# Two of the five taps of a depthwise convolution as matmuls with diagonal weights

## The chip, the cores and the metric

The kernel runs on one core of one Trainium2 chip. Its time is the device time of one execution in microseconds (us). PE is TensorE, DVE is VectorE, ACT is ScalarE, POOL is GpSimd, SP issues the DMAs. PSUM is the memory that matmuls write; the kernel divides it into banks of 128 partitions by 512 float32 values.

## The reference

One layer of a hybrid encoder for 2048 tokens of width 1024: a modulated RMSNorm, one input projection, then two branches side by side (a state-space branch "S5" and a gated DeltaNet branch), an output projection, the residual and a final RMSNorm. The change lies in the DeltaNet branch, where queries, keys and values pass a centred convolution of five taps along the tokens, each channel by itself, and a SiLU:

```python
def centred_depthwise_conv(t, w):            # w: (5, 1536), one weight per tap and channel
    ch = t.shape[-1]
    return lax.conv_general_dilated(
        t, w[:, None, :].astype(t.dtype), window_strides=(1,),
        padding=[(CONV_K // 2, CONV_K // 2)],
        dimension_numbers=("NWC", "WIO", "NWC"), feature_group_count=ch)

proj = h @ w_in
u_a, z_a, qkv, z_b, beta_fb, alpha_fb = jnp.split(proj, [o1, o2, o3, o4, o5], axis=-1)
qkv = jax.nn.silu(centred_depthwise_conv(qkv, conv_w))
q, k, v = jnp.split(qkv, 3, axis=-1)
```

Keys and queries are then normalised per head of 128 channels; the rest of the branch runs later in the kernel.

## The kernel before, in words

The program has three parts in time: a start (norm, modulation, the first columns of the projection), the projection stage, which is the one that the change touches (about 250 to 745 us of the trace), and the DeltaNet chunks with the output projection after it.

In the projection stage the columns of `w_in` are done as jobs of 128 columns: three gate jobs, one job of 16 columns, four key jobs (K1 to K4, `kind` 1), four query jobs (Q1 to Q4, `kind` 0), and then value jobs (V1 to V4, `kind` 2) that alternate with gate jobs (Z). A job has four rounds, one for each block of 512 tokens. A round is one product of 24 float16 matmuls of 128x512 into a bank `gm` (three for each of eight slices of the 1024 inputs: high parts, and the two cross terms with the low parts), the eviction by ACT, and one `tick`.

The order of everything else is written out by hand: each engine works through its instructions in the order in which the Python code emits them. `later(n, f, rank)` puts `f` into the n-th tick from now; a tick runs what is due, sorted by rank, and then one step of `side`, a generator that carries the S5 branch along: first its parameters (long chains of small DVE operations), then eight tables (`s5_tables`: transposes `sq<-ident,bpw` and small products `sq<-cpw,bbr` and `sq<-cpw,bbi`), then sixteen batches (`s5_in`: `sq<-uT,bpt` and four DVE products; in the next tick `s5_out` of the batch before: `sq<-uT,tt` and `sq<-w,cpt`, and `s5_scan`: four DVE scans into `xs` and three DVE operations, the first of which writes a bank).

For each block a key, query or value job runs: `evac` (ACT copies the product, scaled, into `raw`, which holds 2048 tokens with two zeros at either end), two ticks later `tap` (ACT writes `raw` times the first tap's weight into `cv`), one tick later `conv` (DVE adds four taps by `scalar_tensor_tensor`, the first three results in a PSUM bank, the last in `cv`), one tick later `gated` (SiLU). Keys go on through `total` (sum of squares by matmuls), `taken`, a `rsqrt` chain on DVE once per job, and `turn` (transposes), values through `turn`.

Banks come from one pool: two with the tag `gm`, three `pt`, three `sq`. The convolution shares the three `sq` banks with the S5 tables and batches; a matmul into a bank whose last reader has not finished waits, and so does all of PE behind it. The weights of the next job are split into `wh` (ACT) and `wl` (DVE, line 223) while the present one runs.

Of the kernel before, what the change touches and what calls it, by code (L numbers as in the profile page):

```python
# [9 lines left out]
F32 = mybir.dt.float32  # L10
# [5 lines left out]
AF = mybir.ActivationFunctionType  # L16
# [15 lines left out]
def mm(nc, out, lhsT, rhs, start=True, stop=True):  # L32
    nc.tensor.matmul(out, lhsT, rhs, start=start, stop=stop)  # L33


def bc(ap, n):
    return ap.unsqueeze(2).to_broadcast([ap.shape[0], ap.shape[1], n])
# [3 lines left out]
def block(ctx, tc, x, c, ada_w, ada_b, norm_w, w_in, conv_w,  # L41
# [4 lines left out]
    nc = tc.nc  # L46
    V, A, P = nc.vector, nc.scalar, nc.gpsimd
# [28 lines left out]
    def select(name, src, pattern, base, cm, op=ALU.is_ge):  # L76
        t = const.tile([128, 128], F32, name=name)
        P.affine_select(out=t, in_=src, pattern=pattern, compare_op=op, fill=0.0, base=base, channel_multiplier=cm)
        return t

    def pool(name, bufs=1, side="left", **kw):
        return tc.tile_pool(name=name, bufs=bufs, side=side, reuse_waits="tile", **kw)
# [4 lines left out]
    def bank(tag, shape=(128, 512)):  # L87
        return psum.tile(list(shape), F32, tag=tag, name=tag, bufs=PS_BUFS[tag])

    ident = select("ident", ones, [[-1, 128]], 0, 1, op=ALU.is_equal)  # L90
# [17 lines left out]
    def rsqrt(pool, dst, src, tag):  # L108

        shp = list(src.shape)  # L110
        y = pool.tile(shp, F32, tag=tag + "y", name=tag + "y")
        t = pool.tile(shp, F32, tag=tag + "t", name=tag + "t")
        V.tensor_scalar(out=t.bitcast(I32), in0=src.bitcast(I32), scalar1=1, scalar2=None,
                        op0=ALU.arith_shift_right)
        V.tensor_scalar(out=y.bitcast(I32), in0=t.bitcast(I32), scalar1=-1.0,
                        scalar2=float(0x5F3759DF), op0=ALU.mult, op1=ALU.add)
        for it in range(3):
            V.tensor_tensor(out=t, in0=y, in1=y, op=ALU.mult)
            V.scalar_tensor_tensor(out=t, in0=t, scalar=-0.5, in1=src, op0=ALU.mult, op1=ALU.mult)
            V.scalar_tensor_tensor(out=(dst if it == 2 else y), in0=t, scalar=1.5, in1=y,  # L120
                                   op0=ALU.add, op1=ALU.mult)
# [52 lines left out]
    cw = s5t.tile([128, 12, 5], F32, name="cw")  # L174
# [794 lines left out]
    tp = p1.enter_context(pool("tp", 2))  # L969
# [5 lines left out]
    def later(n, fn, rank=0):  # L975
        late.append((clock[0] + n, fn, rank))
# [9 lines left out]
    def job(i, evac):  # L986
        w = w_done(i)
        for tb in range(NB):
            ps = gemm(w, tb)
            evac(tb, ps, w[2])  # L990
            if tb == 0:
                w_dma(i + 2)
                mx, cut = w_max(i + 1), w_cut(i + 1)
                next(mx, None)
            elif tb == 1:
                whole(mx)
            else:
                next(cut, None)
                next(cut, None)
            tick()  # L1000
# [8 lines left out]
    def conv_job(i, kind, h):  # L1009
        i12 = kind * 4 + h  # L1010
        raw = rp.tile([128, L + 4], F32, tag="big", name="raw")
        V.memset(raw[:, 0:2], 0.0)
        V.memset(raw[:, L + 2:L + 4], 0.0)
        cvs = {}
        if kind == 1:
            ss, rk = [sp.tile([128, NCH], F32, tag=t, name=t, bufs=2) for t in ("kss", "rk")]

        def evac(tb, ps, iv):
            A.activation(out=raw[:, 2 + tb * 512:2 + (tb + 1) * 512], in_=ps, func=AF.Copy, scale=iv)  # L1019
            if tb:  # L1020
                later(1, lambda: tap(tb - 1))
            if tb == NB - 1:
                later(2, lambda: tap(tb))

        def tap(tb):
            cv = cvs[tb] = tp.tile([128, 512], F32, tag="cv", name="cv", bufs=9)
            A.activation(out=cv, in_=raw[:, tb * 512:tb * 512 + 512], func=AF.Copy, scale=cw[:, i12, 0:1])  # L1027
            later(1, lambda: conv(tb))

        def conv(tb):  # L1030

            cv, ps = cvs[tb], bank("sq")
            o = tb * 512
            for j in range(1, 5):
                V.scalar_tensor_tensor(out=cv if j == 4 else ps, in0=raw[:, o + j:o + j + 512],  # L1035
                                       scalar=cw[:, i12, j:j + 1], in1=cv if j == 1 else ps,
                                       op0=ALU.mult, op1=ALU.add)
            later(1, lambda: gated(tb))

        def gated(tb):  # L1040
            cv = cvs[tb]
            A.activation(out=cv, in_=cv, func=AF.Silu)
            if kind == 0:
                nc.sync.dma_start(out=qT_d[:, tb * 4:tb * 4 + 4, h, :], in_=cv.rearrange("p (c t) -> p c t", t=128))
            if kind == 2:
                later(1, lambda: turn(tb))
                return
            sq = tp.tile([128, 512], F32, tag="sq", name="sq")
            A.activation(out=sq, in_=cv, func=AF.Square)
            later(1, lambda: total(tb, sq), 2)  # L1050

        def total(tb, sq):

            ps = bank("pt")
            for j in range(4):
                mm(nc, ps[:, j:j + 1], sq[:, j * 128:(j + 1) * 128], ones[:, 0:1])
            later(1, lambda: taken(tb, ps), 1)

        def taken(tb, ps):
            c4 = slice(tb * 4, tb * 4 + 4)  # L1060
            if kind == 0:

                V.tensor_scalar(out=iq2[:, c4, h], in0=ps[:, 0:4], scalar1=EPS, scalar2=128.0 * EPS,
                                op0=ALU.add, op1=ALU.mult)
                cvs.pop(tb)
                return
            V.tensor_scalar(out=ss[:, c4], in0=ps[:, 0:4], scalar1=EPS, scalar2=None, op0=ALU.add)
            if tb == NB - 1:

                rsqrt(sp, rk, ss, "rk")  # L1070
                for n in range(NB):
                    later(1 + n, lambda n=n: turn(n), 2)

        def turn(tb):
            c4 = slice(tb * 4, tb * 4 + 4)
            cv = cvs.pop(tb)
            ps = bank("pt")
            for j in range(4):
                nc.tensor.transpose(ps[:, j * 128:(j + 1) * 128], cv[:, j * 128:(j + 1) * 128], ident)  # L1079
            if kind == 2:  # L1080
                vt = tp.tile([128, 4, 128], F32, tag="z", name="vt", bufs=3)
                A.activation(out=vt, in_=ps, func=AF.Copy)
                nc.sync.dma_start(out=vt_d[:, c4, h, :], in_=vt)
                return
            later(1, lambda: norm(ps, c4), 1)

        def norm(ps, c4):
            kt = tp.tile([128, 4, 128], F32, tag="kt", name="kt", bufs=3)
            V.tensor_tensor(out=kt, in0=ps.rearrange("p (c d) -> p c d", d=128), in1=bc(rk[:, c4], 128), op=ALU.mult)
            nc.sync.dma_start(out=kt_d[:, c4, h, :], in_=kt)  # L1090
            later(2, lambda: back(kt, c4), 1.5)

        def back(kt, c4):
            ps = bank("pt")
            for j in range(4):
                nc.tensor.transpose(ps[:, j * 128:(j + 1) * 128], kt[:, j, :], ident)
            kk = tp.tile([128, 4, 128], F32, tag="z", name="kk", bufs=3)
            A.activation(out=kk, in_=ps, func=AF.Copy)
            nc.sync.dma_start(out=kT_d[:, c4, h, :], in_=kk)

        job(i, evac)

    def ab_job(i):
# [162 lines left out]
    for c0, n in order[NU:]:  # L1266
        if (c0, n) in ZA:
            z_job(i, za_d[:, ZA.index((c0, n)), :])
        elif (c0, n) in ZB:
            z_job(i, zb_d[:, ZB.index((c0, n)), :])  # L1270
        elif n == 16:
            ab_job(i)
        else:
            kind, h = divmod((c0 - 1024) // 128, 4)
            conv_job(i, kind, h)
        i += 1
# [588 lines left out]
```

## Time and profile before

| | |
|---|---|
| median of 3 runs | 1396.05 us (1393.25 to 1398.34) |
| the profiled execution | 1399.54 us, span of its trace 1397.8 us |
| mean granted TensorE clock | 0.959 |
| PE busy | 1283.2 us, 92% of the span |
| DVE busy | 1000.4 us, 72% |
| ACT busy | 672.1 us, 48% |
| POOL busy | 703.7 us, 50% |

A busy time is the sum over one engine's instructions, overlaps counted once. Matmuls are pipelined: each is shown longer than the distance to the next one, so the pace of PE is read from the distance between starts. PEld is the loading of the stationary operand, which runs beside the matmuls. PEclk is the clock that TensorE was granted as a share of its full speed. In a timeline each row has its start, its length, engine, line, operation, output and inputs, shape and count, and in brackets the idle time before it with what ended it.

### The profile page before, as it was taken

To read this page: it belongs to the slowest core of one execution; us is meant where nothing else is said; L and a number is where in the kernel's file an instruction comes from. 1 tells how busy PE (TensorE), PEld (TensorE's weight loads), DVE (VectorE), ACT (ScalarE), POOL (GpSimd) and SP (SyncE) were. 2 spreads that over 40 slices of the span, in tenths; PEclk is the share of its full clock that TensorE was granted. 3 is DMA by queue.
4 is the path that set the end of the run, shared out by engine and by line. 5 is a ranking of instruction groups with operands and counts; after the bars stand their busy time and mean duration, and the time that the engine had idled before them with its cause. 6 is when DMAs were issued, how large, how long until landed. Compare 5 with 4: busy or idle time off the path is not lost.

```text
span 1397.8 us, 26533 instructions
## 1 busy us (share of the span) xinstructions
PE 1283.2 (92%) x9936; PEld 902.9 (65%) x9936; DVE 1000.4 (72%) x2095; ACT 672.1 (48%) x1348; POOL 703.7 (50%) x680
## 2 busy tenths in 40 slices
PE   2879897898999999999998789999999988998997
PEld 2445343354665555555554679999998877887885
DVE  4636479877765899889865677888888555865664
ACT  4445321444654555344446566777666423432332
POOL 3214223655541478878731765656653235654443
PEclk9789998999999999999999899999999999999998
DMA  9445342222457434353525423444435487686533
GB/s 313 169 93 180 96 83 84 66 80 83 117 170 186 134 113 144 91 163 100 150 74 150 147 77 116 152 145 138 132 111 197 144 289 276 226 309 211 181 111 108
DMA packets 255280, 206.43 MB, mean 148 GB/s; under 512 B 88496, under 2 KB 206256, under 8 KB 255152
## 3 DMA queue, kind: packets, MB, share of 16 engines
q1 hardware_dynamic: 255152, 204.75, 47.5%
q8 instruction: 78, 1.28, 0.4%
q14 instruction: 50, 0.41, 0.1%
HBM read 133.38 MB, written 73.33 MB: 148 GB/s over the span
## 4 chain that ended last, share of the span: by engine, by line
PE 70%; DVE 16%; DMA 4%; issue 3%; ACT 2%; POOL 2%; SPq 1%; DVEq 0%; POOLq 0%; ACTq 0%
PE gm L33 38%; PE sq L33 16%; PE pt L33 12%; DVE sq L1035 3%; DVE w L510 1%; DVE tm L510 1%; DVE xs L939 1%; PE pt L1079 1%; DMA of<-o_d 1%; DVE t L510 1%; DVE wl L223 1%; PE sq L1752 1%; DMA xt<-in_x_dram 1%; DMA ay_d<-ytx 1%; DVE pb L1423 0%
## 5 line engine op out<-in xcount | busy, mean ns | idle before, releaser
L33 PE MATMUL gm<-hhi,wh 128*128 128x512 f16 (+1 forms) x784 | 294.3, 392 | 14.7 <-ACT wh L221 8.2
L33 PE MATMUL gm<-hhi,wl 128*128 128x512 f16 (+1 forms) x784 | 293.1, 390 | 8.8 <-DVE wl L223 8.8
L33 PE MATMUL gm<-hlo,wh 128*128 128x512 f16 (+1 forms) x784 | 293.3, 391 | 0.0
L33 PEld LDWEIGHTS <-wh 128*128 128x128 f16 (+1 forms) x1664 | 154.0, 101 | 200.6 <-issue 25.3
L33 PEld LDWEIGHTS <-wl 128*128 128x128 f16 (+1 forms) x832 | 79.7, 100 | 106.7 <-DVE wl L223 11.4
L1019 ACT ACTIVATE raw<-gm,w 128x512 f32<-128x512 f32 x48 | 33.1, 690 | 177.6 <-PE gm L33 177.6
L510 POOL TENSOR_TENSOR w<-w,w 128x512 f32<-128x512 f32 x32 | 50.1, 1575 | 83.3 <-DVE w L510 83.3
L33 PE MATMUL gm<-yh,gwh 128*128 128x256 f32 x256 | 80.4, 314 | 6.4 <-ACT yh L778 5.4
L1035 DVE SCALAR_TENSOR_TENSOR sq<-raw,cw,sq 128x512 f32<-128x512 f32 x96 | 72.6, 756 | 3.4
L33 PE MATMUL gm<-yl,gwh 128*128 128x256 f32 x256 | 73.7, 288 | 0.7 <-POOL yl L779 0.7
L1774 POOL TENSOR_TENSOR r<-r,xt 128x512 f32<-128x512 f32 x32 | 41.4, 1295 | 63.5 <-DVE r L1773 31.0
L33 PE MATMUL gm<-yh,gwl 128*128 128x256 f32 x256 | 72.9, 285 | 0.0
L1035 DVE SCALAR_TENSOR_TENSOR sq<-raw,cw,cv 128x512 f32<-128x512 f32 x48 | 50.7, 1057 | 29.3 <-ACT cv L1027 28.7
L1444 ACT ACTIVATE Y<-pt 128x512 f16<-128x512 f32 x96 | 58.0, 604 | 27.1 <-PE pt L33 26.4
L33 PE MATMUL sq<-S,kq 128*128 128x128 f32 x480 | 64.1, 287 | 0.0
L33 PEld LDWEIGHTS sq<-S,kq 128*128 128x128 f32 x480 | 61.7, 201 | 2.0
L1005 ACT ACTIVATE z<-gm,w 128x512 f32<-128x512 f32 x32 | 22.0, 688 | 84.6 <-PE gm L33 49.7
L1423 DVE CAST_PREDICATED pb<-msk,pt 128x512 f16<-128x512 int8 x80 | 56.9, 714 | 6.6 <-PE pt L33 5.4
L939 DVE TENSOR_TENSOR_SCAN xs<-c,w 128x255 f32<-128x255 f32 x64 | 61.1, 1013 | 0.6 <-POOL w L510 0.6
L33 PE MATMUL pt<-Y,nh 128*128 128x64 f16 (+1 forms) x896 | 56.5, 198 | 5.4 <-DVE Y L1431 5.1
L320 POOL TENSOR_SCALAR hhi<-hf 128x512 f16<-128x512 f32 x32 | 30.0, 957 | 55.0 <-ACT hf L318 47.9
L1445 ACT ACTIVATE YT<-pt 128x512 f16<-128x512 f32 x96 | 57.3, 597 | 0.0
(456 smaller groups left out, 3529.8 us busy)
## 6 DMA issues: line engine op xcount, KB each, us to landing
xt<-in_x_dram SPq DMA_DIRECT2D x25, 512.0 KB
ws<-in_w_in_dram SPq DMA_DIRECT2D x24, 512.0 KB
aw<-in_ada_w_dram SPq DMA_DIRECT2D x24, 512.0 KB
kq<-kT_d SPq DMA_DIRECT2D x32, 256.0 KB
kq<-qT_d SPq DMA_DIRECT2D x32, 256.0 KB
kt<-kt_d SPq DMA_DIRECT2D x32, 256.0 KB
vt<-vt_d SPq DMA_DIRECT2D x32, 256.0 KB
out_dram<-r SPq DMA_DIRECT2D x16, 512.0 KB
```

The costliest lines, as they stand in the source:

```text
L33: nc.tensor.matmul(out, lhsT, rhs, start=start, stop=stop)
L223: V.scalar_tensor_tensor(out=wl, in0=ws, scalar=s, in1=wh, op0=ALU.mult, op1=ALU.subtract)
L320: P.tensor_scalar(out=hhi[:, k, sl], in0=hf, scalar1=1.0, scalar2=1.0, op0=ALU.mult, op1=ALU.mult)
L510: (e or V).tensor_tensor(out=o, in0=a, in1=b, op=op)
L939: V.tensor_tensor_scan(out=o, data0=m1, data1=v, initial=0.0, op0=ALU.mult, op1=ALU.add)
L1005: A.activation(out=z, in_=ps, func=AF.Silu, scale=iv)
L1019: A.activation(out=raw[:, 2 + tb * 512:2 + (tb + 1) * 512], in_=ps, func=AF.Copy, scale=iv)
L1035: V.scalar_tensor_tensor(out=cv if j == 4 else ps, in0=raw[:, o + j:o + j + 512], scalar=cw[:, i12, j:j + 1], in1=cv if j == 1 else ps, op ...
L1423: V.copy_predicated(out=cols(PB[d][li], b, d), mask=mb, data=pp.rearrange("p t (n b) -> p t n b", b=b))
L1444: A.activation(out=cols(Y[d], b, d), in_=pa.rearrange("p t (n b) -> p t n b", b=b), func=AF.Copy)
L1445: A.activation(out=cols(YT[d], b, 1 - d), in_=pb.rearrange("p t (n b) -> p t n b", b=b), func=AF.Copy)
L1774: P.tensor_tensor(out=r[:, ns], in0=r[:, ns], in1=xt[:, ns], op=ALU.add)
```

## The change

In the eight key and value jobs (`kind` 1 and 2) the taps 0 and 1 are done by PE: at the start of the job ACT writes two diagonal matrices `dg` (identity times the tap's weight per channel), and in the tick where ACT did tap 0 before, two float32 matmuls of 128x512 accumulate the two taps in a bank `sq`. One tick later DVE adds the taps 2, 3 and 4 onto that bank, three operations in place of four. The query jobs stay as they were. `tap` gets rank 2 there, so it comes after the `conv` of the block before in the same tick. The buffers of `cv` go from 9 to 8, and `dg` takes two of its own.

```diff
+        NP = 2 if kind else 0
+        if NP:
+            dg = tp.tile([128, NP, 128], F32, tag="dg", name="dg")
+            for j in range(NP):
+                A.activation(out=dg[:, j], in_=ident, func=AF.Copy, scale=cw[:, i12, j:j + 1])

         def evac(tb, ps, iv):
             A.activation(out=raw[:, 2 + tb * 512:2 + (tb + 1) * 512], in_=ps, func=AF.Copy, scale=iv)
+            if NP:
+                later(2, lambda: tap(tb), 2)
+                later(3, lambda: conv(tb))
+                return
...
         def tap(tb):
-            cv = cvs[tb] = tp.tile([128, 512], F32, tag="cv", name="cv", bufs=9)
+            if NP:
+                cvs[tb] = ps = bank("sq")
+                for j in range(NP):
+                    mm(nc, ps, dg[:, j], raw[:, tb * 512 + j:tb * 512 + j + 512], j == 0, j == NP - 1)
+                return
+            cv = cvs[tb] = tp.tile([128, 512], F32, tag="cv", name="cv", bufs=8)
...
         def conv(tb):
-            cv, ps = cvs[tb], bank("sq")
+            if NP:
+                ps, cv = cvs[tb], tp.tile([128, 512], F32, tag="cv", name="cv", bufs=8)
+                cvs[tb] = cv
+            else:
+                cv, ps = cvs[tb], bank("sq")
             o = tb * 512
-            for j in range(1, 5):
+            for j in range(max(NP, 1), 5):
                 V.scalar_tensor_tensor(out=cv if j == 4 else ps, in0=raw[:, o + j:o + j + 512],
                                        scalar=cw[:, i12, j:j + 1], in1=ps if NP or j > 1 else cv,
                                        op0=ALU.mult, op1=ALU.add)
```

A bank is now taken in the tick of `tap` and held until the end of `conv` one tick later; before, it was taken and given back by `conv` alone. How this changes the order is shown at two places. The names: `dg` the diagonals, `sq` the banks with that tag, `cpw`, `bbr` and `bbi` the operands of an S5 table, `xs` the scans, `rt` a table of rotations; "waits" names the engines (or DMA queues) whose semaphores the instruction waits for.

PE in the third round of K1, before: behind the round's last matmul stand the sixteen small products of a table, eight into one bank and eight into another.

```order
L33 MATMUL gm<-hhi,wl 128x512
L33 MATMUL sq<-cpw_2397,bbr 32x128 [waits Activation_49,Pool_49]
L33 MATMUL sq<-cpw_2398,bbi 32x128 [waits Pool_49]
...
L33 MATMUL sq<-cpw_2397,bbr 32x128 [waits Activation_49]
L33 MATMUL sq<-cpw_2398,bbi 32x128
```

The same place now:

```order
L33 MATMUL gm<-hhi,wl 128x512
L33 MATMUL sq<-raw,dg 128x512 [waits Activation_49]
L33 MATMUL sq<-raw,dg 128x512
L33 MATMUL sq<-cpw_2397,bbr 32x128 [waits Activation_49,Pool_49]
L33 MATMUL sq<-cpw_2398,bbi 32x128 [waits Pool_49]
...
L33 MATMUL sq<-cpw_2397,bbr 32x128 [waits DVE_49]
L33 MATMUL sq<-cpw_2398,bbi 32x128
```

The two diagonal matmuls of K1's second block stand ahead of the table, and the table's second bank is now the one that the first block's taps hold, so its first matmul waits for DVE, which reads that bank in `conv`.

DVE in the fourth round of V2, before: the S5 products, the convolution of the second block, the scans and the write into a bank.

```order
L510 TENSOR_TENSOR w_5788<-sq,rt_5511 128x512 [waits DMAHW3_49,DMAHW2_49,Activation_49]
L223 SCALAR_TENSOR_TENSOR wl<-ws,w_5630,wh 128x1024 [waits DMAHW5_49,Activation_49]
L1035 SCALAR_TENSOR_TENSOR sq<-raw,cw,cv 128x512 [waits DVE_49,Activation_49]
L1035 SCALAR_TENSOR_TENSOR sq<-raw,cw,sq 128x512 [waits DVE_49] x2
L1035 SCALAR_TENSOR_TENSOR cv<-raw,cw,sq 128x512 [waits DVE_49]
L939 SCALAR_TENSOR_TENSOR xs_4424<-c_1467,w_5785 128x255 [waits Pool_49]
...
L510 TENSOR_TENSOR sq<-xs_4424,rt_5510 128x512 [waits DVE_49]
```

The same place now:

```order
L510 TENSOR_TENSOR w_5807<-sq,rt_5526 128x512 [waits DMAHW3_49,DMAHW2_49,Activation_49]
L223 SCALAR_TENSOR_TENSOR wl<-ws,w_5648,wh 128x1024 [waits DMAHW5_49,Activation_49]
L1053 SCALAR_TENSOR_TENSOR sq<-raw,cw,sq 128x512
L1053 SCALAR_TENSOR_TENSOR sq<-raw,cw,sq 128x512 [waits DVE_49]
L1053 SCALAR_TENSOR_TENSOR cv<-raw,cw,sq 128x512 [waits DVE_49]
L939 SCALAR_TENSOR_TENSOR xs_4436<-c_1467,w_5804 128x255 [waits Pool_49]
...
L510 TENSOR_TENSOR sq<-xs_4436,rt_5525 128x512 [waits DVE_49,Activation_49]
```

The operation with two inputs in SBUF (`raw` and `cv`) is gone, and the bank that the scans' result is written into is now one that ACT reads last (the output of `s5_out`), so DVE waits for ACT there.

More of the change, by code (lines that the diff above doesn't have):

```diff
@@ L1030, in conv @@
         def conv(tb):
-            cv, ps = cvs[tb], bank("sq")
+            if NP:
[3 more added lines that the diff above has]
+                cv, ps = cvs[tb], bank("sq")
             o = tb * 512
-            for j in range(1, 5):
+            for j in range(max(NP, 1), 5):
                 V.scalar_tensor_tensor(out=cv if j == 4 else ps, in0=raw[:, o + j:o + j + 512],
-                                       scalar=cw[:, i12, j:j + 1], in1=cv if j == 1 else ps,
+                                       scalar=cw[:, i12, j:j + 1], in1=ps if NP or j > 1 else cv,
                                        op0=ALU.mult, op1=ALU.add)
```

## The prediction

> **What bounds the kernel now.** I read first the page's busy times and its chain of work, then a table of busy time by stretches, then the timelines of PE and DVE at the places where PE stands idle.
>
> ```profile
> PE 1283.2 (92%) x9936; PEld 902.9 (65%) x9936; DVE 1000.4 (72%) x2095; ACT 672.1 (48%) x1348; POOL 703.7 (50%) x680
> PE 70%; DVE 16%; DMA 4%; issue 3%; ACT 2%; POOL 2%; SPq 1%; DVEq 0%; POOLq 0%; ACTq 0%
> core 0: us, PE busy (x) PEld busy (x) DVE busy (x) ACT busy (x) POOL busy (x), PEclk, DMA share, GB/s
> 260.00:300.00 40.00, 33.52 (x226) 17.35 (x225) 34.81 (x90) 15.91 (x32) 24.57 (x23) 0.91 0.24 73
> 300.00:340.00 40.00, 36.11 (x217) 20.47 (x216) 27.97 (x43) 19.86 (x42) 21.97 (x23) 0.91 0.19 55
> 340.00:465.00 125.00, 124.04 (x834) 73.88 (x832) 83.55 (x172) 65.73 (x129) 49.80 (x54) 1.00 0.62 169
> 465.00:545.00 80.00, 80.00 (x474) 45.62 (x472) 76.04 (x110) 43.67 (x71) 62.02 (x53) 1.00 0.37 108
> 545.00:745.00 200.00, 199.95 (x1116) 105.65 (x1115) 159.48 (x214) 92.14 (x148) 136.18 (x112) 1.00 0.41 126
> ```
>
> The last five rows are the stage of the change. From 340 to 745 us PE is busy for 404.0 of 405 us at the full clock, so in the value jobs and in the later key rounds every microsecond of new PE work lengthens the stage. From 260 to 340 PE stands idle for 10.4 us and has the clock at 0.91; there DVE is what it waits for. DVE is nearly full from 465 to 545 (76.04 of 80), but PE has no gap beside it, so DVE ends nothing there.
>
> **What is added: 64 float32 matmuls of 128x512.** Two per block, 16 key and 16 value blocks. The start of the kernel has two of exactly this form (the gate: `pt<-accg,ones`), in the midst of float16 matmuls:
>
> ```profile
> 163.28 0.38 PE L33 MATMUL gm<-hhi,wl 128*128 128x512 f16 x1
> 163.49 1.88 PE L33 MATMUL pt<-accg,ones 128*128 128x512 f32 x4
> 165.21 0.38 PE L33 MATMUL gm<-hhi,wh 128*128 128x512 f16 x1
> ```
>
> Two float32 matmuls are four records, and the stream behind them starts 165.21 - 163.49 = 1.72 us later (0.43 a record; a float16 one takes 163.49 - 163.28 = 0.21). So a block costs PE 1.72 us, and 32 blocks 55.0 us. The stationary loads lie beside. The least that the nearest other row allows is float16's pace for each of the 128 records, 27 us.
>
> The page "TensorE: Matmul & The Clock Gate" of the Trainium skill, section "Back-to-back issue gap", puts a sustained stream of loads and matmuls at some 131 ns per matmul of 512 columns. The rows here show 0.21 us, so the measurement decides; by the page's figure, an estimate, the 55.0 us would be 33 and the sum about 22 us lower.
>
> **What is removed, all of it off PE.**
>
> ```profile
> L1027 ACT ACTIVATE cv<-raw,cw x48: 705/707/713, 263.2 to 721.7; 128x512 f32<-128x512 f32 x48
> L1035 DVE SCALAR_TENSOR_TENSOR sq<-raw,cw,cv x48: 747/797/1841, 273.5 to 722.5; 128x512 f32<-128x512 f32 x48
> L1035 DVE SCALAR_TENSOR_TENSOR sq<-raw,cw,sq x96: 754/756/757, 275.2 to 724.0; 128x512 f32<-128x512 f32 x96
> L1035 DVE SCALAR_TENSOR_TENSOR cv<-raw,cw,sq x48: 748/748/749, 276.7 to 724.8; 128x512 f32<-128x512 f32 x48
> L1035 DVE SCALAR_TENSOR_TENSOR sq<-raw,cw,cv 128x512 f32<-128x512 f32 x48 | 50.7, 1057 | 29.3 <-ACT cv L1027 28.7
> 259.00 0.30 ACT L859 ACTIVATE lks<-sq 128x128 f32<-128x128 f32 x1
> ```
>
> ACT loses 32 x 0.707 = 22.6 us and gains 16 diagonals at about 0.30 (nearest row: a 128x128 copy), 4.8 us. DVE loses 32 operations of the one form that varies, 32 x 1.057 = 33.8 us, and keeps three of 0.75 per block. Neither engine ends a round after 340 us, so this is worth something only where PE waits for DVE. The fewer `cv` buffers cost nothing that I can see: a key's `cv` is read by `turn` one tick before its buffer comes round again, and it is taken a tick later than before.
>
> **Where PE waits for DVE: the first 90 us of the key jobs.**
>
> ```profile
> 274.75 0.38 PE L33 MATMUL gm<-hlo,wh 128*128 128x512 f16 x1
> 281.61 0.61 PE L33 MATMUL gm<-hhi,wl 128*128 128x512 f16 x1 [6.48 <-DVE wl L223]
> 284.42 0.38 PE L33 MATMUL gm<-hhi,wh 128*128 128x512 f16 x1
> 287.66 0.95 PE L33 MATMUL pt<-ones,sq 128*128 128x1 f32 x8
> 321.23 1.03 PE L33 MATMUL pt<-ones,sq 128*128 128x1 f32 x8
> 326.15 1.12 PE L1079 MATMUL pt<-ident,cv 128*128 128x128 f32 x4 [3.89 <-DVE kss L1067]
> 332.12 0.38 PE L33 MATMUL gm<-hhi,wh 128*128 128x512 f16 x1
> 343.39 1.02 PE L33 MATMUL pt<-ones,sq 128*128 128x1 f32 x8 [0.75 <-DVE raw L1013]
> ```
>
> K2's first product waits 6.48 us for `wl`, and K1's `turn` 3.89 us for the `rsqrt` chain. After each the pace halves for a while: the 7 matmuls from 281.61 to 284.42 take 2.81 us in place of 1.5, and the 4 transposes and 12 matmuls from 326.15 to 332.12 take 5.97 in place of about 3.0. With the 0.75 at 343 these waits cost 6.5 + 1.3 + 3.9 + 3.0 + 0.75 = 15.4 us. Work of PE that comes in front of such a wait is free up to its length, and DVE comes sooner now. But one new wait comes in, in K1's third round:
>
> ```profile
> 262.51 1.07 PE L838 MATMUL sq<-ident,bpw 128*128 128x128 f32 x8
> 268.69 0.50 PE L33 MATMUL sq<-cpw,bbr 64*32 64x128 f32 x16
> 269.34 0.39 PE L33 MATMUL gm<-hhi,wh 128*128 128x512 f16 x1
> 273.49 1.63 DVE L1035 SCALAR_TENSOR_TENSOR sq<-raw,cw,cv 128x512 f32<-128x512 f32 x1
> 276.74 0.75 DVE L1035 SCALAR_TENSOR_TENSOR cv<-raw,cw,sq 128x512 f32<-128x512 f32 x1
> 280.28 1.27 DVE L223 SCALAR_TENSOR_TENSOR wl<-ws,w,wh 128x1024 f16<-128x1024 f32 x1
> ```
>
> The table's second bank is now held by the first block's taps until `conv` has read it. DVE reaches that `conv` at 273.5, behind the S5 parameters, and three operations end at 275.8. PE gets there two taps (3.44 us) later than the 268.69 of the row, with half the table done at 272.4: a wait of 3.5 us. The third round then ends at 281.4. The third block's tap needs the bank of the second, whose `conv` stands behind `wl`; DVE has wl done at 280.6 and that `conv` at 282.9, so PE goes on at 282.9 at the earliest, and K2's first round starts at 284.7 and ends at 289.9, with no wait for `wl`. If the 3.5 us wait halves the pace as the other two did, it ends at 291.2. The row at 287.66 is the same point before: +2.3 to +3.5, and I take +3.0 where three taps are worth 5.2.
>
> Whether 3.5 us are enough for the slow pace no row shows; 3.89 were, and 0.75 were not. The same page of the Trainium skill, section "The HAM clock gate (the "warmup" mystery)", says the half clock comes after an idle window of about 3.4 us of a free-running counter; the two waits in the rows agree, and by that rule a wait of 3.5 us would rarely fill a window, which makes +2.3 the likelier end.
>
> **The sum.** At K2's first round +3.0. Six more taps up to K1's `turn`: 10.3. There the wait and the slow pace behind it (6.9) vanish, since PE comes at 321.23 + 1.0 + 13.3 = 335.5, while DVE's chain, which begins when a key block's sums are taken, shifts by four or five taps only and is done some 7 us ahead. So +6.4; less the 0.75; seven more key taps, 12.0: +17.7 at the end of the key jobs. Sixteen value blocks, PE being full: 27.5. Together +45.2 us. On the profiled execution, span 1397.8, that is 1443.0, and 1399.5 becomes 1444.7; that execution lay 3.5 above the median of the runs, so I give 1396.05 + 45.2 = **1441 us**. The query jobs, the start and what follows 745 us only shift.
>
> **The value rounds in detail**, since a matmul can wait for a bank there too:
>
> ```profile
> 570.25 1.11 PE L33 MATMUL sq<-uT,tt 128*128 128x256 f32 x4
> 571.29 2.00 PE L33 MATMUL sq<-w,cpt 64*128 64x256 f32 x16
> 578.51 1.95 PE L33 MATMUL sq<-uT,bpt 128*64 128x256 f32 x16
> 567.17 4.75 DVE L939 TENSOR_TENSOR_SCAN xs<-c,w 128x255 f32<-128x255 f32 x4 [0.19 <-POOL w L510]
> 571.84 1.04 DVE L510 TENSOR_TENSOR sq<-xs,rt 128x512 f32<-128x512 f32 x1
> 573.93 0.69 DVE L510 TENSOR_TENSOR w<-sq,w 128x512 f32<-128x512 f32 x1
> 573.32 0.66 ACT L965 ACTIVATE w<-sq 128x256 f32<-128x256 f32 x2 [1.40 <-PE sq L33]
> ```
>
> In V2's second round the tap moves `s5_out` and ACT's reading of its first bank from 573.3 to 575.0, and that ends at 575.4. DVE, done with the scans at 571.8, now waits for that bank, 3.5 us; its three operations end at 578.3, small operations behind them about 1 us later, and `conv` at 581.6. On PE the next tap ends at 582.0 (578.51 + 2 x 1.72), and the matmul that wants `conv`'s bank, half-way through the batch's 1.95 us, comes 0.9 later: it is in time by 1.3 us. A late DVE catches up: of the 159 us that it is busy from 545 to 745, 12 blocks' 1.06 go, and the stretch grows by 12 taps, which leaves it at 147 of 221 us. I cost these waits at 0, with 1.5 us in each of the 8 rounds with a batch's start as the upper end, 12 us.
>
> **Rivals.** (a) The key jobs give nothing back: PE's waits there come back as waits for banks, and all 55.0 us show, 1451; for it speaks the new wait that already took 3.5 us. (b) Banks bind: three `sq` banks, each held a round longer. If the margin of 1.3 us fails in most rounds, say 24 of 32 by 1.5 us, 36 us come on top: 1477. Against it stands DVE's slack of a third; for it, that the removed form is not the only one that varies (scans of 4.75 us here). (c) The other side, not slower: PE's busy time hides short waits, its records being longer (0.38) than their pace (0.21), and rounds really end on DVE, whose share of the chain is 16%. Then the 33.8 us taken off DVE would be gained and the taps fall into the hidden waits: 1396 - 34 = 1362. It decides where the hidden waits reach 1.72 us a block, but two such starts with nothing else between lie 0.21 apart, which leaves no room. (d) The matmuls run faster than the gate's rows, at the float16 pace: 27.5 us in place of 55.0, +18: 1414. The figure of 131 ns on the Trainium skill's page named above would lie between this and the forecast.
>
> **How the numbers follow.** Forecast 0.74, own range 1431 to 1450 (clock and waits of the key jobs 5 us either way, runs 2.5, value waits up to 5). (a) 0.14, (b) 0.07, (c) 0.02, (d) 0.03. Leaving out (b), (c) and (d), 0.12, and widening for (a) and the 12 us of value waits, the range is 1427 to 1457. A measurement of this kernel tells a change from none at about 0.3%, 4 us. Only (c) gives faster, and nothing sits within 4 us but a mishap: faster 0.02, same 0.01, slower 0.97.
>
> **What would show it.** In the profile after: rows `sq<-raw,dg`, 128 records at 0.43 apart; a stage that ends near 790 in place of 745; PE full from 350 on; no wait for `wl` near 282 but one for DVE ahead of the table; DVE's mean of the removed form gone and its idle time larger; DVE waiting for ACT ahead of the scans' bank write. I am wrong if the taps show another pace, if PE shows waits in the value rounds, or if the part after the stage changes length.

## The result, and the profile after

| | before | after |
|---|---|---|
| median | 1396.35 us (1393.25 to 1398.34, 4 runs) | 1441.84 us (1439.97 to 1442.70, 4 runs) |
| ratio, with its 95% interval | | 1.0321 (1.0304 to 1.0337) |
| profiled execution, its span | 1399.54, 1397.8 us | 1442.70, 1441.0 us |
| mean granted TensorE clock | 0.959 | 0.965 |

The change costs 45.5 us. On the page of after, in the order of before, first the busy times and the chain that ended last; then the windows by stage, with the columns as before:

```profile
PE 1338.8 (93%) x10064; PEld 928.6 (64%) x10064; DVE 963.6 (67%) x2063; ACT 657.7 (46%) x1332; POOL 693.4 (48%) x680
...
PE 77%; DVE 9%; DMA 3%; issue 3%; ACT 2%; POOL 2%; SPq 1%; DVEq 0%; POOLq 0%; ACTq 0%
```

```profile
260.00:300.00 40.00, 38.15 (x202) 18.94 (x200) 27.05 (x88) 15.80 (x41) 22.10 (x22) 1.00 0.24 72
300.00:340.00 40.00, 40.00 (x256) 21.78 (x255) 21.04 (x39) 14.10 (x34) 20.82 (x22) 1.00 0.18 53
340.00:480.00 140.00, 139.64 (x890) 82.16 (x889) 78.14 (x164) 66.88 (x131) 50.10 (x56) 1.00 0.54 148
480.00:560.00 80.00, 80.00 (x447) 44.23 (x446) 68.97 (x103) 37.66 (x62) 54.91 (x47) 1.00 0.37 106
560.00:790.00 230.00, 230.00 (x1217) 120.00 (x1216) 151.73 (x208) 90.23 (x149) 136.27 (x118) 1.00 0.37 112
```

PE is 55.6 us busier, DVE 36.8 and ACT 14.4 us less busy, and the chain has moved from DVE (16 to 9%) to PE (70 to 77%). The hole of 10.4 us that PE had between 260 and 340 is down to 1.85 us, and the clock there has gone from 0.91 to 1.00. From 300 us on PE is full, value rounds included.

The new instructions, by the tile `dg` (shortest, median and longest in ns, first and last start):

```profile
L33 PE MATMUL sq<-raw,dg x128: 592/592/676, 265.3 to 763.9; 128*128 128x512 f32 x128
L1021 ACT ACTIVATE dg<-ident,cw x16: 384/401/405, 256.5 to 722.6; 128x128 f32<-128x128 f32 x16
```

PE's timeline in the first key jobs:

```profile
265.30 1.96 PE L33 MATMUL sq<-raw,dg 128*128 128x512 f32 x4
...
273.15 1.88 PE L33 MATMUL sq<-raw,dg 128*128 128x512 f32 x4
274.96 0.50 PE L33 MATMUL sq<-cpw,bbr 64*32 64x128 f32 x16
...
282.81 1.96 PE L33 MATMUL sq<-raw,dg 128*128 128x512 f32 x4 [1.85 <-DVE raw L1013]
284.60 0.38 PE L33 MATMUL gm<-hhi,wh 128*128 128x512 f16 x1
...
289.78 1.88 PE L33 MATMUL sq<-raw,dg 128*128 128x512 f32 x4
```

The table at 274.96 starts without a wait and its second half follows without one, where one of 3.5 us was forecast. The third block's tap waits 1.85 us (the row names DVE's clearing of K2's `raw`, which ended last; it stands right behind the `conv` that holds the bank), and the waits for `wl`, for `kss` and at 343 are gone.

The starts of ACT's evictions measure each part. Here are K1's first, Q1's second (all key taps are done by then), the last one ahead of the first value tap, and one at the stage's end; first four rows of before, then four of after:

```profile
256.96 0.69 ACT L1019 ACTIVATE raw<-gm,w 128x512 f32<-128x512 f32 x1 [1.55 <-PE gm L33]
387.43 0.69 ACT L1019 ACTIVATE raw<-gm,w 128x512 f32<-128x512 f32 x1 [2.79 <-PE gm L33]
504.51 0.69 ACT L1019 ACTIVATE raw<-gm,w 128x512 f32<-128x512 f32 x1 [2.71 <-PE gm L33]
725.70 0.69 ACT L1005 ACTIVATE z<-gm,w 128x512 f32<-128x512 f32 x1 [2.28 <-PE gm L33]
```

```profile
259.74 0.69 ACT L1024 ACTIVATE raw<-gm,w 128x512 f32<-128x512 f32 x1 [2.52 <-PE gm L33]
403.94 0.69 ACT L1024 ACTIVATE raw<-gm,w 128x512 f32<-128x512 f32 x1 [4.53 <-PE gm L33]
521.13 0.69 ACT L1024 ACTIVATE raw<-gm,w 128x512 f32<-128x512 f32 x1 [2.70 <-PE gm L33]
769.67 0.69 ACT L1005 ACTIVATE z<-gm,w 128x512 f32<-128x512 f32 x1 [4.61 <-PE gm L33]
```

The shifts are +2.78, +16.51, +16.62 and +43.97 us. So 2.78 us were there before any tap ran, the key jobs cost 16.51 - 2.78 = 13.73, the queries 0.11, together 13.84, and the values 43.97 - 16.62 = 27.35.

### The profile page after: what moved, and what is told of

It is laid out like the page before. It is cut to its first block, busy times and chain, and to the rows that moved or that the text cites. A ratio compares the mean times of both kernels' runs of the same rounds, so it can differ in the third digit from the quotient of the medians.

```text
span 1441.0 us, 26754 instructions
## 1 busy us (share of the span) xinstructions
PE 1338.8 (93%) x10064; PEld 928.6 (64%) x10064; DVE 963.6 (67%) x2063; ACT 657.7 (46%) x1332; POOL 693.4 (48%) x680
## 4 chain that ended last, share of the span: by engine, by line
PE 77%; DVE 9%; DMA 3%; issue 3%; ACT 2%; POOL 2%; SPq 1%; DVEq 0%; POOLq 0%; ACTq 0%
PE gm L33 41%; PE sq L33 20%; PE pt L33 13%; PE pt L1097 1%; DVE tm L510 1%; DMA of<-o_d 1%; DVE pb L1441 1%; DVE YT L1454 1%; DMA xt<-in_x_dram 1%; PE sq L1770 1%; DVE wl L223 0%; PE pt L1114 0%; DVE r L1802 0%; DVE z L1532 0%; POOL ra L1714 0%
## 5 line engine op out<-in xcount | busy, mean ns | idle before, releaser
L510 DVE TENSOR_TENSOR w<-sq,rt 128x512 f32<-128x512 f32 x64 | 41.0, 685 | 42.9 <-PE sq L33 42.9
L33 PE MATMUL sq<-raw,dg 128*128 128x512 f32 x128 | 60.8, 598 | 1.8 <-DVE raw L1013 1.8
L223 DVE SCALAR_TENSOR_TENSOR wl<-ws,w,wh 128x1024 f16<-128x1024 f32 (+1 forms) x25 | 35.0, 1402 | 35.6 <-ACT wh L221 33.3
```

The costliest lines, as they stand in the source:

```text
L223: V.scalar_tensor_tensor(out=wl, in0=ws, scalar=s, in1=wh, op0=ALU.mult, op1=ALU.subtract)
L510: (e or V).tensor_tensor(out=o, in0=a, in1=b, op=op)
```

## The experiments

All parts below are counted in this way: keys (with the queries behind them) from the first to the third of those evictions, values from the third to the fourth, each less the same stretch in the first profile of before. The last column is the difference of medians on one chip.

| kernel | PE time of the taps, us a block | keys | values | median less before |
|---|---|---|---|---|
| before, second profile | 0 | -1.6 | 0.0 | |
| the change | 1.72 | 13.8 | 27.35 | +45.5 |
| keys alone | 1.72 | 13.9 | 0.0 | +15.0 |
| values alone | 1.72 in values | -1.6 | 27.35 | +27.3 |
| taps twice | 3.43 | 39.3 | 54.8 | +97.9 |
| taps in F32R | 0.47 | -0.2 | 9.6 | +10.6 |
| bank held, no matmul | 0 | -4.1 | 22.1 | +20.2 |
| one tap | 0.86 | 10.1 | 16.8 | +24.1 |
| change with GpSimd kept busy | 1.72 | 20.7 | 27.35 | +51.4 |
| change with `wl` early | 1.72 | 20.5 | 27.35 | +47.3 |
| before with `wl` early | 0 | -5.5 | 0.0 | -6.3 |
| before with `wl` early, `turn` late | 0 | -11.9 | 0.0 | -8.8 |

**Half of the change at a time.** The theory is that of the prediction: the loss is PE's time, less the waits in the key jobs that it fills. The rival is that holding the banks longer costs a good part of it.

```diff
-        NP = 2 if kind else 0
+        NP = 2 if kind == 1 else 0        # keys alone; kind == 2: values alone
```

> The diagonals in the key jobs alone; values as before. Theory P (the cost is the float32 matmuls' own time on PE, less the waits of the key jobs that they fill): 16 x 1.72 = 27.5 us less about 14 us of waits, so +13.7 us on the kernel before, as the traces shift between K1 and the end of the key jobs: 1410 us, 1407 to 1413. Rival B (holding a bank a round longer is what costs, PE waiting for DVE): the key part would keep its waits, +25 us or more: 1421.

> The diagonals in the value jobs alone; keys as before. Theory P: PE is full there, 16 x 1.72 = 27.5 us with no relief: 1424 us, 1421 to 1427, and no wait of PE in the value rounds. Rival B: more than 30 us, with waits of PE for DVE ahead of the diagonals or of a batch's products.

Keys alone take 1413.00 us, the upper end of theory P's range, ratio 1.0115 (1.0091 to 1.0140), +15.0; values alone 1425.26, ratio 1.0196 (1.0181 to 1.0211), +27.3. The halves add up: 42.3 of the 45.5, within the intervals. Sixteen value blocks at 1.72 are 27.5, and 27.35 are measured.

**The taps twice.**

```diff
-                for j in range(NP):
+                for j in 2 * list(range(NP)):
                     mm(nc, ps, dg[:, j], raw[:, tb * 512 + j:tb * 512 + j + 512], j == 0, j == NP - 1)
```

> Each pair of diagonal matmuls issued twice into the same bank (the second pair starts the sum anew; the result is the same). Theory P: 64 more matmuls with no wait left to fill, 55.0 us on the changed kernel: 1497 us, 1494 to 1500. Rival B: the bank's release and not PE's time sets the end, so the second pair fits partly into waits: under 1485.

It takes 1495.85 us, within theory P's range, ratio 1.0701 (1.0680 to 1.0723): +97.9, 52.4 more than the change. Sixteen value blocks cost 54.8 us, 3.43 each. The keys grow by 25.4 of 27.5 us, since the last wait of 1.85 us is filled now too. Once the key waits are full, each tap costs its whole time.

**A cheaper form of matmul.** `raw` and `dg` are declared F32R, a rounded float32, for keys and values; the full precision of the taps is left out.

```diff
+        fr = F32R if kind else F32
-        raw = rp.tile([128, L + 4], F32, tag="big", name="raw")
+        raw = rp.tile([128, L + 4], fr, tag="big", name="raw")
...
-            dg = tp.tile([128, NP, 128], F32, tag="dg", name="dg")
+            dg = tp.tile([128, NP, 128], F32R, tag="dg", name="dg")
```

> All 64 diagonal matmuls as in the changed kernel, same banks, same order, but diagonals and raw in the type F32R (rounded), so that a 128x512 matmul is one record at the pace of the float16 ones, 0.21 us, instead of two at 0.43. Theory P: the 55.0 us shrink to 64 x 0.215 = 13.8, the relief of the key jobs stays: between -3 and +4 us on the kernel before, 1393 to 1400. Rival B: banks are held as long as in the changed kernel, so at least half of the +45 us stays: 1420 or more. Inputs of the taps are rounded, which leaves precision out.

It takes 1408.54 us, ratio 1.0078 (1.0060 to 1.0095), +10.6: neither theory's number. The tile `dg` and the waits of PE from 250 to 800 us (total, times, longest):

```profile
L33 PE MATMUL sq<-raw,dg x64: 392/475/767, 265.9 to 732.9; 128*128 128x512 f32 x64
```

```profile
PE sq L33 <- DVE raw L1014: 5.9, 1, 5.9
...
PE sq L33 <- DVE cv L1054: 1.1, 5, 0.3
```

A matmul is one record now, and the shift grows by 0.47 us in a block without a wait: 7.5 in the values, where 9.6 are measured, with five short waits for `conv`'s bank. In the keys the wait for `wl` did not go, it came back as one of 5.9 us for the bank of the block before, whose `conv` stands behind `wl` on DVE. With the full taps it is 4.1 us shorter, and 2.5 of these are the longer work of the two blocks' taps in front of it. PE's time explains most of the loss, and a rest of 2 us in the values points at the banks.

**The bank held, without any matmul.** ACT writes tap 0 straight into the bank, in the tick where the matmuls stood, and DVE does the other four on it.

```diff
-        NP = 2 if kind else 0
+        NP = 1 if kind else 0
...
-                for j in range(NP):
-                    mm(nc, ps, dg[:, j], raw[:, tb * 512 + j:tb * 512 + j + 512], j == 0, j == NP - 1)
+                A.activation(out=ps, in_=raw[:, tb * 512:tb * 512 + 512], func=AF.Copy, scale=cw[:, i12, 0:1])
```

> No matmuls: ScalarE writes the first tap of keys and values straight into the PSUM bank, in the tick where the matmuls stood, and VectorE adds the other four taps on that bank. The bank is taken and held as long as in the change, without its work on TensorE. Theory P (the loss is the time of the matmuls, holding the banks longer is nearly free): 1391 to 1400, within 0.4% of the kernel before; VectorE's first operation falls from a mean of about 1.06 us to 0.75. Theory B (the longer hold of the banks costs TensorE its order and is a large part of the 45 us): 1410 or more.

It takes 1418.56 us, ratio 1.0144 (1.0125 to 1.0162): theory P's number fails, and all of it is lost in the values, 22.1 us. The waits of PE from 500 to 800 us, PE's timeline at the worst of them, and DVE's operation that it waits for:

```profile
PE sq L33 <- DVE cv L1050: 9.7, 7, 2.0
```

```profile
584.13 1.78 PE L33 MATMUL sq<-uT,bpt 128*64 128x256 f32 x8 [1.89 <-DVE cv L1050]
585.84 0.61 PE L33 MATMUL gm<-hhi,wh 128*128 128x512 f16 x1
586.24 0.63 PE L33 MATMUL gm<-hlo,wh 128*128 128x512 f16 x1
...
604.43 1.61 PE L33 MATMUL sq<-uT,bpt 128*64 128x256 f32 x8 [1.99 <-DVE cv L1050]
```

```profile
583.33 0.75 DVE L1050 SCALAR_TENSOR_TENSOR cv<-raw,cw,sq 128x512 f32<-128x512 f32 x1
```

The batch's matmul wants the bank that `conv` holds, comes 1.9 us too early, and a slow pace follows (0.42 a matmul in place of 0.21). So the longer hold has a price where PE has no work of its own ahead of that matmul; with the change's taps PE comes 3.4 us later there and the wait is gone. The column of values shows both: 0, 0.47, 0.86, 1.72 and 3.43 us of taps a block cost 22.1, 9.6, 16.8, 27.35 and 54.8 us, so hold and matmuls do not add. Of the 22.1 us, 9.7 are such waits, and much of the rest is the slow pace behind them: in the two rounds shown the shift grows by 8.4 us for 4.6 us of waits. One thing only this kernel has, DVE's wait for ACT's writing of the bank. It comes to 18.7 us in the whole kernel but to 0.4 from 500 to 800 us, so it does not explain the loss in the values. In the first round shown DVE waits 1.81 us for ACT's reading ahead of the scans' bank write, which belongs to the new order of the banks, and works without a gap from there (576.39) to the end of `conv`.

**One tap by a matmul, four by DVE** (`NP = 1 if kind else 0`, else the change).

> Only tap 0 of keys and values by a matmul with a diagonal (0.86 us of TensorE a block in place of 1.72); VectorE adds four taps on the bank, all with the bank as an input. Theory M (in each round TensorE pays its own added time or the lateness of the bank, whichever is larger): the value rounds lie between 13.8, TensorE's time alone, and 17, with at most 2 us of waits for banks, the key rounds between 0 and +5; 1411 to 1419. Theory A (the longer hold of the banks and the matmuls add up): 13.8 and the 22 us that the hold alone cost in the values, 1430 or more.

It takes 1422.42 us, ratio 1.0179 (1.0160 to 1.0198), between the two ranges. The values follow theory M, 16.8 us for 13.8 of work. The miss is in the keys, +10.1 in the profiled execution, the slowest of its runs (1421.43 to 1427.46). First DVE's clearing of K1's `raw`, then PE:

```profile
262.56 0.06 DVE L1012 MEMSET raw<- 128x2 f32 x1
```

```profile
276.48 0.68 PE L33 MATMUL sq<-cpw,bbr 64*32 64x128 f32 x8 [3.08 <-DVE cv L1053]
...
288.87 1.60 PE L33 MATMUL sq<-raw,dg 128*128 128x512 f32 x2 [3.56 <-DVE raw L1013]
```

Here is the wait ahead of the table's second bank that the prediction had put into the change. Why it comes in one kernel and not in another is the next question.

**Before, a second time.** The same kernel, unchanged.

> The kernel before, unchanged, profiled a second time. What it tells apart is where the start of its execution lies: in the first profile ScalarE's eviction of K1's first round began at 256.96 us, in the five changed kernels so far 1.7 to 3.6 us later, though nothing of the change has run by then. If the start varies from one execution to the next, this profile has that eviction 1 to 4 us later than 256.96 too, and the differences of the changed kernels are to be counted from that point. If the change itself moved the start, it lies within 0.5 us of 256.96. In both cases product K2 waits about 6.5 us for wl and K1's turn about 3.9 us.

Its run takes 1400.97 us; K1's first eviction starts at 262.01 us, 5.05 later than in the first profile, and later than the 1 to 4 us expected. So the start varies by itself, and the parts are rightly counted from that eviction. The wait for `wl` was expected at 6.5 us and is 5.11; the one for `kss` is 3.89 again. In the first profile DVE clears K1's `raw` (the operation ahead of its S5 chain) at 260.29, 3.3 us after that eviction; in the second at 263.62, 1.6 after it. Rows of the first profile, POOL and DVE, then of the second:

```profile
263.23 1.12 POOL L510 TENSOR_TENSOR bpw<-pwbr,bsr 128x512 f32<-128x512 f32 x1 [3.26 <-PE sq L838]
```

```profile
260.29 0.06 DVE L1012 MEMSET raw<- 128x2 f32 x1
...
265.47 1.28 DVE L510 TENSOR_TENSOR t<-su 128x32 f32<-128x32 f32 x1
```

```profile
268.28 1.06 POOL L510 TENSOR_TENSOR bpw<-pwbr,bsr 128x512 f32<-128x512 f32 x1 [3.22 <-PE sq L838]
```

```profile
263.62 0.06 DVE L1012 MEMSET raw<- 128x2 f32 x1
...
267.97 0.19 DVE L510 TENSOR_TENSOR t<-t,t 128x32 f32<-128x32 f32 x1
268.41 0.97 DVE L510 TENSOR_TENSOR cu<-cu,t 128x32 f32<-128x32 f32 x1
...
271.63 1.63 DVE L1035 SCALAR_TENSOR_TENSOR sq<-raw,cw,cv 128x512 f32<-128x512 f32 x1
```

As soon as POOL starts on the next table, many of DVE's small operations go from 0.19 to about 1 us. In the second profile all but the last few are done by then, and from the clearing to `conv`'s first operation it is 8.0 us; in the first they meet half-way, and it is 273.49 - 260.29 = 13.2. A lateness of 1.7 us at the start had become 7. The profile with one tap has the late start too: DVE clears `raw` at 262.56, 3.3 us after the eviction at 259.23. In the eleven other profiles of this document it is 1.6. So that kernel's miss in the keys goes with a late start, and its three other runs lie 4.8 us or more below the profiled one.

**GpSimd kept busy.** To make that a cause and not a coincidence, the changed kernel gets four more products on POOL in the gap where it sat idle.

```diff
+        if gb == 0:
+            t = sc_.tile(shp, F32, tag="tp0", name="tmp", bufs=1)
+            for _ in range(4):
+                TT(t, pb_[0], bw[0], ALU.mult, P)
         nc.sync.dma_start(out=lk_d[gb], in_=lks)
```

> The changed kernel, with four more products of 128x512 on GpSimd (about 1.06 us each, into a scratch tile that nobody reads) right behind its two small additions at 262.6 us, where it sat idle for 5.0 us. VectorE's code is the same. Theory C (VectorE's small operations become slow while GpSimd works, and the wait for the table's bank did not come because the two did not meet): a good part of the some 20 operations of 0.18 to 0.35 us between 262.9 and 266.3 take about 1 us, conv of K1's first block ends 3 to 6 us later than the 269.7 of the changed kernel (counted from K1's first eviction), TensorE waits 1 to 4 us for it ahead of the table's second bank, and the time is 1442 to 1447. Theory D (in the profile of before VectorE was late for another reason): these operations stay at 0.18 to 0.35, conv ends within 1 us of where it did, no new wait, 1440 to 1443.

It takes 1449.66 us, ratio 1.0376 (1.0356 to 1.0397), +51.4 where the change has +45.5, and 2.7 above the range. POOL, DVE and PE there:

```profile
263.22 4.63 POOL L510 TENSOR_TENSOR tmp<-pwbr,bsr 128x512 f32<-128x512 f32 x4
```

```profile
263.26 1.06 DVE L671 TENSOR_SCALAR su<-den 128x32 f32<-128x32 f32 x1
...
277.72 0.75 DVE L1057 SCALAR_TENSOR_TENSOR cv<-raw,cw,sq 128x512 f32<-128x512 f32 x1
```

```profile
278.52 0.68 PE L33 MATMUL sq<-cpw,bbr 64*32 64x128 f32 x8 [2.43 <-DVE cv L1057]
...
280.39 0.63 PE L33 MATMUL gm<-hhi,wl 128*128 128x512 f16 x1
```

Theory C holds: DVE's code is the same, many of its operations are slow from the moment POOL starts, `conv` of the first block ends 8 us later than in the change, counted from the eviction and more than expected, PE waits 2.43 us for it, and the pace halves. The key jobs cost 20.7 us in place of 13.8.

The Trainium skill, page "SBUF — State Buffer", section "Who interferes with whom", says that a VectorE instruction with two SBUF inputs and a GpSimd instruction that reads SBUF exclude one another, the first holding the port for its whole length. The trace agrees on operations with two inputs: what DVE loses on one, up to about 1.1 us, is about the length of one POOL product. It also shows an operation with one input slowed (`su<-den`, 1.06 us), which that sentence does not cover.

**Without the waits that the taps filled.** Before, with K2's `wh` and `wl` one round earlier; then also `turn` one tick later.

```diff
             elif tb == 1:
                 whole(mx)
+                if order[i] == KC[0]:
+                    next(cut)
...
-                    later(1 + n, lambda n=n: turn(n), 2)
+                    later(2 + n, lambda n=n: turn(n), 2)      # second kernel only
```

> The kernel before, with one thing moved: in K1 alone the steps that make the next job's weights (wh, wl) come one round earlier, ahead of the S5 parameters on VectorE. Theory F (the first wait of the key jobs is worth its full length, so the taps filled it and gave it back): the 6.48 us wait for wl at 281.6 and the 1.3 us of slow pace behind it vanish: 1396 less 7.8, 1386 to 1391. Theory W (VectorE is late there by itself, so the wait comes back as a wait for a bank or the next transposes, as it did with the faster matmuls): 1393 to 1398, with a wait for a bank of 4 to 7 us in the same round.

> As the last, and the key jobs' turn (four transposes behind the rsqrt chain) one tick later in addition. Theory F: both waits and their slow pace vanish, 7.8 and 6.9 us: 1396 less 14.7 is 1381; since the turns now fall into rounds of the next job where something else may be late, 1379 to 1388. Theory W: the waits come back elsewhere, 1391 to 1398. If the first wait comes back and the second doesn't, 1386 to 1391.

The first takes 1392.09 us, ratio 0.9954 (0.9940 to 0.9968); the second 1389.64, ratio 0.9937 (0.9923 to 0.9952). PE's wait in the first:

```profile
280.45 0.39 PE L33 MATMUL gm<-hhi,wl 128*128 128x512 f16 x1 [1.78 <-DVE wl L223]
```

Of 6.48 us (5.11 in the second profile) 1.78 are left, with no slow pace behind and no wait for a bank in its place. The key jobs shrink by 5.5 and 11.9 us, 3.9 and 10.3 against the second profile of before, and the second kernel has no wait for `kss`. Theory F has the mechanism, but its sizes, 7.8 and 14.7 us, are not reached: the medians fall by 6.3 and 8.8. The second kernel's 10 to 12 us are most of what the change's key jobs did not pay (27.5 less 13.8, or less 15.4 against the second profile). These two versions beat both kernels, by less than 1%, and they have no matmul for the taps.

**The change with `wl` early** (the edit to `cut` alone).

> The changed kernel, with K2's wh and wl made one round earlier, as in the kernel before with that move alone, which gained 6 us. Theory P (the taps fill that wait, so there is nothing left to gain): the end of the key jobs lies 12 to 14 us above the kernel before, counted from K1's first eviction, as in the changed kernel (13.7), and the time is 1439 to 1442. Theory G (what the key rounds gave back came from elsewhere, and the move gains the same here): 1434 to 1437.

It takes 1445.59 us (1442.64 to 1452.28), ratio 1.0354 (1.0319 to 1.0388). Theory G's gain is not there, and theory P's numbers are missed on the other side. DVE and PE:

```profile
273.75 1.28 DVE L223 SCALAR_TENSOR_TENSOR wl<-ws,w,wh 128x1024 f16<-128x1024 f32 x1 [5.06 <-ACT wh L221]
```

```profile
277.33 0.45 PE L33 MATMUL sq<-cpw,bbr 64*32 64x128 f32 x8 [3.07 <-DVE cv L1055]
```

The moved `wl` now stands ahead of the first block's `conv` and waits 5.06 us for ACT's `wh`. In the kernel before, PE did not wait for that `conv`; with the taps the table's second bank hangs on it. The edit that gains 6.3 us in one kernel gains nothing in the other. In the profiled run it loses 6.6 us in the keys, but two of the four runs lie at 1442.7, as the change does, so a loss is not shown.

## Why the prediction was right, and where not

Forecast 1441 us, measured 1441.84; +45.2 and +45.5. Point by point:

- **1.72 us a block.** Right. In the value rounds the shift grows by 1.71 to 1.72 a block; 27.5 against 27.35, and 54.8 with the taps twice.
- **The removed work is worth nothing off PE.** Right in the values. A diagonal was put at 0.30 us by a copy of the same size and took 0.40, 6.4 us for sixteen in place of 4.8, hidden.
- **The key jobs: +17.7, measured 13.84.** The term that failed is the first, K2's first round at +3.0: it is -0.66 (289.78 after less 287.66 before, less the 2.78 of the start). The forecast wait of 3.5 us at the table did not come. That a held bank can make PE wait for `conv` there is right, as the runs with one tap, with taps and `wl` early, and with POOL busy show (3.08, 3.07 and 2.43 us). But the prediction took the instant at which DVE reaches that `conv`, 273.5 in the first profile, as fixed, and two things move it. One is the start, which was late there by chance. The other is the tap itself, which the prediction overlooked: POOL's next table waits for transposes (`sq<-ident,bpw`) that stand behind the first block's taps on PE. In the profile after it starts 8.04 us behind the eviction, in both profiles of before 6.27, and DVE has already begun that `conv` (267.37) when it does:

```profile
267.78 1.06 POOL L510 TENSOR_TENSOR bpw<-pwbr,bsr 128x512 f32<-128x512 f32 x1 [4.99 <-PE sq L838]
```

  By an estimate from these rows the wait would not have come with the late start either. POOL would start 8.04 - 3.33 = 4.71 us after DVE's clearing, about as in the second profile of before (4.66), where `conv` began 8.0 us after it; with its three operations (2.4 us) it would end at 259.74 + 3.33 + 8.0 + 2.4 = 273.5, and PE asks for the bank at about 275.3. No run shows that case. What followed was sized well: to the end of K1's `turn` +3.4 forecast, +3.37 measured; from there to the end of the key jobs 11.3 forecast, 11.1 measured (with the queries).
- **Against the usual before** the key jobs cost 13.84 + 1.6 = 15.4, since the first profile's were the longer ones (the kernel with values alone, whose key jobs are those of before, has -1.6 too); with the values that is 42.8 of the 45.5. The rest lies within the scatter of the runs (5 us before, 2.7 after) and was not located.
- **The value rounds at 0, in time by 1.3 us.** Right. In V2's second round DVE waits 3.54 us for ACT's reading ahead of the scans' bank write, where 3.5 were forecast (2.6 on the mean of 8 rounds); `conv` ends at 605.2, and PE asks for its bank at about 606.3, in time by 1.1 us. DVE waits for the taps too. PE has two waits of 0.2 us from 340 to 800 us, and DVE these:

```profile
DVE sq L510 <- ACT w L965: 20.4, 8, 4.8
DVE sq L1053 <- PE sq L33: 16.0, 4, 5.9
```

  The margin of 1.3 us stood on two taps of 1.72 that delay PE. Without them PE would be 3.44 - 1.3 = 2.1 too early, and the kernel with the bank held and no matmul waits 1.89 and 1.99. That the numbers lie so close is partly luck: DVE does four operations on the bank there, and no tap delays `s5_out`.
- **The rivals.** (a) needed the waits to come back as waits for banks. In the change only 1.85 us did; with POOL busy more did, and the key jobs cost 20.7 of 27.5. (b), the banks, shows only in kernels whose taps take 0.86 us a block or less. (Its 4.75 us are the length of four scans, not of one.) (c) had DVE end the rounds; with 37 us taken off it, every value block still costs the taps' 1.72. (d) had a cheaper record, which the change's matmuls have not; where F32R gave it, the time fell to 1408.5.

## What to carry to other kernels

Where one engine is full, cost moved work at that engine's whole pace, and look at each of its waits separately: work put ahead of a wait is free up to its length, while an earlier instruction on the late engine removes the wait for nothing. When a buffer is held longer, compute the margin of the next user with and without the new work, since the same hold cost nothing here beside 1.72 us of matmuls and 22 us beside none. A forecast wait that hangs on one instant of one profile should be checked against a second profile, and it should be asked whether the new work moves that instant too.

## What the runs showed of the hardware

- Two 128x512 float32 matmuls take four records and 1.72 us, one F32R matmul one record; a block of two costs 0.47 us.
- Many VectorE operations of 128x32 go from 0.18 us to between 0.9 and 1.3 while GpSimd works, one-input ones too (1.06 us for `su<-den`); 1.7 us of lateness became 7.
- The pace of PE halved after waits of 1.89 us (584.13, granted clock 0.57 from 584 to 588) and 2.43 us (278.52, 0.52 from 278 to 285), but not after 1.85 (282.81), 1.78 (280.45) or 2.66 (290.13, with POOL busy) (the prediction took 3.5 for a borderline). The Trainium skill, page "TensorE: Matmul & The Clock Gate", section "The HAM clock gate (the "warmup" mystery)", has the half clock come after an idle window of about 3.4 us; here shorter waits brought it on, so the measurement decides, and whether a wait does so cannot be told from its length alone.
